# Top-k threshold search of a sparse attention: the count of each search's largest block moved from VectorE to ScalarE

## The chip, the cores and the metric

The kernel runs on one core of a Trainium2 chip. The metric is the device time of one execution in microseconds (us); lower is better. DVE is VectorE, ACT is ScalarE, PE is TensorE, POOL is GpSimd, SP is SyncE with its DMA queue.

## The reference, cut to what matters

Two layers on a sequence of 1024 tokens with 1024 channels in float32. Layer 0 is a sparse attention: an indexer gives each query a score for every key it may see, the 256 best keys are kept, and attention runs over these. Layer 1 is a retention; each layer ends with a gated convolutional FFN. The part that bears on the change:

```python
    topk = min(TOPK_MAX, seq // 4)                                  # 256
    def block(args):
        qb, qib, wb, tb = args
        limit = (tb // CHUNK + 1) * CHUNK
        admissible = key_pos[None, :] < limit[:, None]
        rel = jax.nn.relu(jnp.einsum('bqhd,bsd->bqhs', qib, ki).astype(jnp.float32))
        score = jnp.einsum('bqhs,bqh->bqs', rel, wb.astype(jnp.float32))
        score = jnp.where(admissible[None], score, -jnp.inf)
        _, idx = lax.top_k(score, topk)
        ...
        logits = jnp.where(valid[:, :, None, :], logits, -jnp.inf)
        p = jax.nn.softmax(logits, axis=-1).astype(v_sel.dtype)
        return jnp.einsum('bqhk,bqkd->bqhd', p, v_sel)
```

Equal scores are taken in the order of their index, as `top_k` does.

## The kernel before, in words

Queries lie in 8 blocks of 128 (one per partition); block b sees the first 128 (b + 1) keys. Blocks 0 and 1 see at most 256 keys and need no search. The tokens are worked on in two halves of 512: `in_proj` projects half 0, then half 1, and `indexer` (L369) makes the scores of blocks 2 and 3 beside the first and of blocks 4 to 7 beside the second. Per head and segment of keys it issues two matmuls, a Relu on ACT into a temporary (L380), and a DVE operation that weights it into the score tile `sc` (L383 for the first head, L385 for the others).

`topk` (L391) does not gather. It finds for each query the bits of the 256th largest score: in 31 iterations, from bit 30 to bit 0, every block's scores are compared with the threshold and counted (`count`, L404 to L407: one DVE instruction per block that writes the comparison to `junk` and the sum to `cnt`, with a short accumulator read behind it). Then two small DVE steps on one column per block make the bit (L416, tile `tkb`) and the next threshold (L417, tile `tkt`). One more count stands ahead of the loop (against zero, for the sign, L411) and one behind it (strictly above, L418). The rest (L420 to L429) marks ties by a scan and turns the scores into an additive mask, in place.

There are two searches: a for blocks 2 and 3 (384 and 512 keys), b for blocks 4 to 7 (640, 768, 896 and 1024 keys). Both are generators. A function `steps(n)` advances the first of a list of generators by n yields; the code calls it between projections (`steps((3, 10)[half])`, L268; L246, L255, L332 likewise) for search a, and for search b in the output projection of half 0 (`steps(5)`, L1198) and in the first FFN products (`steps(3)`, L1208). Attention on blocks 0 to 3 (L1196) is written between the two. That is the order in which the code asks for the work. The order in which each engine's queue holds it is made by the framework (`schedule_with_timeline_sim=True`, L1325) from that order, the data dependencies and its own estimate of times; then each engine runs its queue in order.

Weights come by DMA as float32 (`wprep`, L80 to L90), ACT makes their upper half (L87), POOL or DVE the lower half (L89). Matmuls run three times per tile, on halves (`mm3`, L121; `product`, L748). Results in PSUM are split in the same way (`split_psum`, L127: ACT L131 or L134, DVE L132 or L135). POOL also makes the lower halves of squares (L233), inverse square roots (L139) and the scaling of the softmax (L503); the attention's maxima are DVE's (L490), its exponentials ACT's (L501). The sum in `square_sum` (L174), the normaliser (L739) and the FFN's input split (L730, L731) follow the output projection (L552).

Of the kernel before, what the change touches and what calls it, by code (L numbers as in the profile page):

```python
# [5 lines left out]
F32 = mybir.dt.float32  # L6
F32R = mybir.dt.float32r
F16 = mybir.dt.float16
I32 = mybir.dt.int32
AF = mybir.ActivationFunctionType  # L10
ALU = mybir.AluOpType
PSUM = bass.MemoryType.PSUM
# [11 lines left out]
TOPK = 256  # L24
INADM = -3.0e38
MASKED = -1.0e30


C_GMIX = 0
# [22 lines left out]
class Prog:  # L52
# [27 lines left out]
    def wprep(self):  # L80
# [5 lines left out]
        nc.sync.dma_start(raw[:, :n], src)  # L86
        nc.scalar.activation(hi[:, :n], raw[:, :n], AF.Copy)  # L87
        eng = nc.gpsimd if on_pool else nc.vector
# [38 lines left out]
    def split_psum(self, hi, lo, ps, scale=None):  # L127

        nc = self.nc
        if scale is None:  # L130
            i = nc.scalar.activation(hi, ps, AF.Copy)  # L131
            j = nc.vector.tensor_tensor(lo, ps, hi.bitcast(F32), ALU.subtract)  # L132
        else:
            i = nc.scalar.activation(hi, ps, AF.Copy, scale=scale)  # L134
            j = nc.vector.scalar_tensor_tensor(lo, ps, scale, hi.bitcast(F32), op0=ALU.mult, op1=ALU.subtract)  # L135
# [29 lines left out]
    def square_sum(self, x, k):  # L165

        nc = self.nc
        if k == 0:
            self.acc = self.tp.tile([128, 512], F32, tag="acc", bufs=1, name="acc")
            nc.scalar.activation(self.acc, x[:, k], AF.Square)  # L170
        else:
            sq = self.tmp()
            nc.scalar.activation(sq, x[:, k], AF.Square)
            nc.vector.tensor_tensor(self.acc, self.acc, sq, ALU.add)  # L174
# [41 lines left out]
    def in_proj(self, half, hh, hl, steps, also=lambda j, q, qs: None):  # L216
# [10 lines left out]
        def squares(ps):  # L227

            n, w = ps.shape
            sq, hi, lo = self.tmp()[:n, :w], self.tmp(F32R)[:n, :w], self.tmp(F32R)[:n, :w]  # L230
            nc.scalar.activation(sq, ps, AF.Square)
            nc.scalar.activation(hi, sq, AF.Copy)
# [136 lines left out]
    def indexer(self, b, qs, t0, masks):  # L369
        nc = self.nc  # L370
        L = 128 * (b + 1)
        o = 128 * ((b * (b + 1) - 6) // 2)
        masks[b] = sc = self.sc[:, o:o + L]
        for h in range(8):
            for (o, n) in self.segs(L):
                ps = self.bank()
                nc.tensor.matmul(ps[:, :n], qs[:, h, t0:t0 + 128], self.KH[:, o:o + n], start=True, stop=False)
                nc.tensor.matmul(ps[:, :n], qs[:, h, t0:t0 + 128], self.KL[:, o:o + n], start=False, stop=True)
                rl = self.tmp()
                nc.scalar.activation(rl[:, :n], ps[:, :n], AF.Relu)  # L380
                w = self.wr[:, b, h:h + 1]
                if h == 0:
                    nc.vector.tensor_scalar(sc[:, o:o + n], rl[:, :n], w, None, op0=ALU.mult)  # L383
                else:
                    nc.vector.scalar_tensor_tensor(sc[:, o:o + n], rl[:, :n], w, sc[:, o:o + n],  # L385
                                                   op0=ALU.mult, op1=ALU.add)
            if h == 7:
                nc.vector.memset(sc[0:64, L - 64:], INADM)
            yield

    def topk(self, tag, scs, junk, eqs):  # L391

        nc = self.nc
        V = nc.vector
        B = len(scs)
        Ls = [sc.shape[1] for sc in scs]
        sml = lambda n, dt=F32: self.stat.tile([128, B], dt, tag=f"k{n}{tag}", name=f"tk{n}")
        cnt, need = sml("c"), sml("n")  # L400
        bit, thr = sml("b", I32), sml("t", I32)
        t = thr.bitcast(F32)

        def count(of, op):  # L404
            for b in range(B):
                V.tensor_scalar(junk[:, :Ls[b]], scs[b], of(b), None, op0=op, op1=ALU.add, accum_out=cnt[:, b:b + 1])  # L406
                yield  # L407

        yield from count(lambda b: 0.0, ALU.is_ge)  # L411
        V.tensor_scalar(bit, cnt, TOPK - 0.5, -1.0, op0=ALU.is_lt, op1=ALU.mult)
        V.tensor_scalar(thr, bit, 1 << 30, None, op0=ALU.bitwise_xor)
        for k in range(30, -1, -1):
            yield from count(lambda b: t[:, b:b + 1], ALU.is_ge)
            V.tensor_scalar(bit, cnt, TOPK - 0.5, float(1 << k), op0=ALU.is_lt, op1=ALU.mult)  # L416
            V.scalar_tensor_tensor(thr, bit, (1 << k) >> 1, thr, op0=ALU.bitwise_xor, op1=ALU.bitwise_xor)  # L417
        yield from count(lambda b: t[:, b:b + 1], ALU.is_gt)  # L418
        V.tensor_scalar(need, cnt, -1.0, float(TOPK), op0=ALU.mult, op1=ALU.add)
        for b in range(B):  # L420
            nth, eq = junk[:, :Ls[b]], eqs[:, :Ls[b]]
            V.tensor_scalar(eq, scs[b], t[:, b:b + 1], None, op0=ALU.is_equal)
            V.tensor_tensor_scan(nth, eq, eq, 0.0, ALU.add, ALU.max)
            yield
            V.scalar_tensor_tensor(eq, nth, need[:, b:b + 1], eq, op0=ALU.is_le, op1=ALU.mult)
            yield
            V.scalar_tensor_tensor(scs[b], scs[b], t[:, b:b + 1], eq, op0=ALU.is_gt, op1=ALU.add)
            nc.scalar.activation(scs[b], scs[b], AF.Copy, bias=MASKED, scale=-MASKED)
            yield  # L429
# [814 lines left out]
def constants():  # L1244
# [23 lines left out]
    m3 = np.zeros((128, 384), f)  # L1268
    m3[:64, 192:256] = MASKED
    m3[:, 256:] = MASKED  # L1270
    inv = f(1.0) / (f(10000.0) ** (np.arange(0, 256, 2, dtype=f) / f(256)))
# [57 lines left out]
```

## Time and profile before

| | |
|---|---|
| median of 3 runs | 2783.84 us (2782.68 to 2783.91) |
| the profiled execution | 2783.58 us |
| its span | 2781.7 us |
| PE busy | 2655.4 us, 95% |
| DVE busy | 1866.9 us, 67% |
| ACT busy | 1096.2 us, 39% |
| POOL busy | 265.2 us, 10% |
| mean granted clock of PE | 0.976 |

The profile is of one execution. The span runs from the first to the last instruction. Busy time counts an engine's instructions; a share over the whole span mixes stages with different limits, so the rows below go by stretches of time, in us from the span's start. A granted clock of 1.00 is 2.4 GHz, 0.50 is 1.2 GHz. An instruction's line is the line of the kernel that issued it, which may be a helper's.

### The profile page before, as it was taken

Reading aid. Unit: us, or ns where it says so; the run is one execution under the profiler, and the core shown is the slowest. Engines: PE = TensorE matmul, PEld = TensorE weight load, DVE = VectorE, ACT = ScalarE, POOL = GpSimd, SP = SyncE. Lnnn points to the kernel's source line nnn. Section 1 sums busy time; section 2 is a strip of 40 time slices with the busy share of each in tenths; the row PEclk is TensorE's granted clock in tenths of the full one; section 3 lists DMA queues with packets and bytes.
Section 4 is the critical chain, followed back from the end, with each engine's and each line's share of the span. In section 5 each row is a group of like instructions: output and inputs, shape, how many; then the busy total and the mean of one; then the engine's idle time right before and its main releaser. Section 6 shows DMA issues by size and latency. Waiting matters only on the chain.

```text
span 2781.7 us, 31410 instructions
## 1 busy us (share of the span) xinstructions
PE 2655.4 (95%) x11888; PEld 2174.3 (78%) x11888; DVE 1866.9 (67%) x2828; ACT 1096.2 (39%) x1552; POOL 265.2 (10%) x193
## 2 busy tenths in 40 slices
PE   8977789998999999999999999999998999999999
PEld 6755567887788877888888888888886888888887
DVE  6889999765988878744544445445447977777632
ACT  6545424663433333323333343323334554454210
POOL 2543234321000000000000000000000000000000
PEclk9988789999999999999999999999999999999999
DMA  5221035204465575422222223223222433337712
GB/s 196 76 73 53 2 98 182 99 20 138 160 212 189 193 261 176 150 63 90 84 84 87 88 83 122 76 84 98 77 76 84 144 107 108 119 106 286 234 59 87
DMA packets 110343, 328.34 MB, mean 118 GB/s; under 512 B 12400, under 2 KB 13808, under 8 KB 110192
## 3 DMA queue, kind: packets, MB, share of 16 engines
q1 hardware_dynamic: 110192, 326.34, 35.6%
q8 instruction: 93, 1.52, 0.2%
q14 instruction: 58, 0.48, 0.1%
HBM read 250.27 MB, written 72.35 MB: 116 GB/s over the span
## 4 chain that ended last, share of the span: by engine, by line
PE 77%; DVE 15%; DMA 4%; issue 2%; ACT 2%; POOL 0%; SPq 0%; DVEq 0%; ACTq 0%; POOLq 0%
PE bank L753 25%; PE bank L123 17%; PE bank L125 17%; PE bank L124 17%; DVE junk L406 5%; DMA gin<-ud 2%; DVE tkb L416 1%; PE bank L534 1%; DVE sc L385 1%; DVE tkt L417 1%; DMA wraw<-in_wf_up 1%; DVE T L731 1%; DVE wlo L731 1%; DVE xo L764 0%; DVE lg L490 0%
## 5 line engine op out<-in xcount | busy, mean ns | idle before, releaser
L87 ACT ACTIVATE whi<-wraw 128x1024 fp32r<-128x1024 f32 (+1 forms) x194 | 205.3, 1058 | 507.7 <-PE bank L124 262.2
L753 PE MATMUL bank<-T,whi 128*128 128x512 f32 x1072 | 337.5, 396 | 21.6 <-ACT T L730 15.0
L753 PE MATMUL bank<-B,whi 128*128 128x512 f32 x1056 | 328.1, 393 | 11.1 <-ACT B L730 4.1
L89 DVE TENSOR_TENSOR wlo<-wraw,whi 128x1024 fp32r<-128x1024 f32 (+1 forms) x151 | 185.8, 1231 | 214.1 <-ACT whi L87 209.0
L124 PE MATMUL bank<-g,whi 128*128 128x512 f32 x704 | 274.1, 390 | 0.0
L123 PE MATMUL bank<-g,whi 128*128 128x512 f32 x704 | 266.5, 392 | 7.5 <-ACT g L730 5.6
L125 PE MATMUL bank<-g,wlo 128*128 128x512 f32 x704 | 272.5, 390 | 0.5 <-DVE wlo L731 0.5
L753 PEld LDWEIGHTS bank<-T,whi 128*128 128x128 f32 x1072 | 203.8, 190 | 71.0 <-ACT T L730 17.1
L730 ACT ACTIVATE whi<-wraw 128x1024 fp32r<-128x1024 f32 (+2 forms) x153 | 145.1, 949 | 267.0 <-PE bank L124 133.1
L753 PEld LDWEIGHTS bank<-B,whi 128*128 128x128 f32 x1056 | 199.9, 190 | 54.8 <-ACT B L730 4.4
L731 DVE TENSOR_TENSOR wlo<-wraw,whi 128x1024 fp32r<-128x1024 f32 (+2 forms) x153 | 165.7, 1083 | 76.5 <-ACT whi L730 76.3
L753 PE MATMUL bank<-T,wlo 128*128 128x512 f32 x536 | 210.3, 394 | 0.0
L753 PE MATMUL bank<-B,wlo 128*128 128x512 f32 x528 | 205.2, 392 | 0.0
L124 PE MATMUL bank<-wlo,hh 128*128 128x512 f32 x512 | 199.3, 389 | 0.0
L125 PE MATMUL bank<-whi,hl 128*128 128x512 f32 x512 | 199.3, 389 | 0.0
L123 PE MATMUL bank<-whi,hh 128*128 128x512 f32 x512 | 198.7, 390 | 0.0
L123 PE MATMUL bank<-hh,whi 128*128 128x512 f32 (+2 forms) x480 | 188.7, 393 | 10.3 <-ACT hh L134 8.3
L124 PE MATMUL bank<-hl,whi 128*128 128x512 f32 (+2 forms) x480 | 186.5, 389 | 0.1
L125 PE MATMUL bank<-hh,wlo 128*128 128x512 f32 (+2 forms) x480 | 186.4, 389 | 0.0
L406 DVE TENSOR_SCALAR_CACHE_REDUCE junk<-sc,tkt 128x640 f16<-128x640 f32 (+1 forms) x192 | 181.3, 944 | 4.4
L764 DVE TENSOR_TENSOR xo<-xo,bank 128x512 f32<-128x512 f32 x128 | 86.7, 685 | 126.8 <-PE bank L125 126.8
L123 PEld LDWEIGHTS bank<-g,whi 128*128 128x128 f32 x704 | 132.2, 188 | 37.6 <-ACT g L730 7.8
(244 smaller groups left out, 5305.6 us busy)
## 6 DMA issues: line engine op xcount, KB each, us to landing
wraw<-in_wf_up SPq DMA_DIRECT2D x113, 512.0 KB, 3.6
ud<-cu SPq DMA_DIRECT2D x88, 512.0 KB, 2.7
gin<-ud SPq DMA_DIRECT2D x88, 512.0 KB, 4.5
wraw<-in_wb_vg SPq DMA_DIRECT2D x64, 512.0 KB, 3.5
wraw<-in_wf_dn SPq DMA_DIRECT2D x48, 384.0 KB, 3.6
wraw<-in_wb_qk SPq DMA_DIRECT2D x32, 512.0 KB, 3.6
wraw<-in_wb_out SPq DMA_DIRECT2D x32, 512.0 KB, 3.5
wraw<-in_wa_in SPq DMA_DIRECT2D x26, 512.0 KB, 4.0
```

The source lines that it names most:

```text
L87: nc.scalar.activation(hi[:, :n], raw[:, :n], AF.Copy)
L89: eng.tensor_tensor(lo[:, :n], raw[:, :n], hi[:, :n].bitcast(F32), ALU.subtract)
L123: mm(ps, ah, bh, start=first, stop=False)
L124: mm(ps, ah, bl, start=False, stop=False)
L125: mm(ps, al, bh, start=False, stop=last)
L385: nc.vector.scalar_tensor_tensor(sc[:, o:o + n], rl[:, :n], w, sc[:, o:o + n], op0=ALU.mult, op1=ALU.add)
L406: V.tensor_scalar(junk[:, :Ls[b]], scs[b], of(b), None, op0=op, op1=ALU.add, accum_out=cnt[:, b:b + 1])
L416: V.tensor_scalar(bit, cnt, TOPK - 0.5, float(1 << k), op0=ALU.is_lt, op1=ALU.mult)
L730: return (self.nc.scalar.activation(hi, raw, AF.Copy), self.nc.vector.tensor_tensor(lo, raw, hi.bitcast(F32), ALU.subtract))
L731: self.nc.vector.tensor_tensor(lo, raw, hi.bitcast(F32), ALU.subtract))
L753: self.nc.tensor.matmul(ps, u, v, start=first and k + i == 0, stop=k == 3 and i == 2, skip_group_check=not (first and last))
L764: self.nc.vector.tensor_tensor(o, a, b, op)
```

## The change

Search and count stay the same in what they find. For the last block of each search (512 keys in a, 1024 in b) the counts of the iterations k = 30 to 1 come from ACT: the sum over the keys of the sign of (score minus threshold) goes to `half`, and a second ACT instruction makes half of it plus half the number of keys, the count, if no score equals the threshold. To make that so, the scores of this block are turned, in place, into a form with an order that floating-point addition keeps and with the lowest bit set, while its lowest byte's own bit is saved in a byte tile; ahead of k = 0 the bit is put back. The threshold's column for the block holds its negative in these iterations (one XOR on the sign bit ahead, one behind). All scores start from -2^-100 and not from 0. DVE counts the other blocks as before, and all of them for k = 0, ahead of the loop and behind it. The yields per iteration fall by one, while the calls of `steps` stay as they are.

```diff
+SHIFT = -2.0 ** -100
...
-                    nc.vector.tensor_scalar(sc[:, o:o + n], rl[:, :n], w, None, op0=ALU.mult)
+                    nc.vector.tensor_scalar(sc[:, o:o + n], rl[:, :n], w, SHIFT, op0=ALU.mult, op1=ALU.add)
...
+        z, L = B - 1, Ls[B - 1]
+        half = self.stat.tile([128, 1], F32, tag=f"kh{tag}", name="tkh")
+        xi = scs[z].bitcast(I32)
+        x0 = scs[z].bitcast(U8)[:, 0::4]
+        low, signs = eqs.bitcast(U8)[:, :L], eqs.bitcast(I8)[:, 1024:1024 + L]
+
+        def count(of, op, to=B):
+            for b in range(to):
                 V.tensor_scalar(junk[:, :Ls[b]], scs[b], of(b), None, op0=op, op1=ALU.add, accum_out=cnt[:, b:b + 1])
                 yield
...
         yield from count(lambda b: 0.0, ALU.is_ge)
         V.tensor_scalar(bit, cnt, TOPK - 0.5, -1.0, op0=ALU.is_lt, op1=ALU.mult)
         V.tensor_scalar(thr, bit, 1 << 30, None, op0=ALU.bitwise_xor)
+        V.tensor_scalar(thr[:, z:], thr[:, z:], -(1 << 31), None, op0=ALU.bitwise_xor)
+        V.tensor_scalar(low, x0, 1, None, op0=ALU.bitwise_and)
+        yield
+        V.tensor_scalar(xi, xi, 1, None, op0=ALU.bitwise_or)
+        V.scalar_tensor_tensor(xi, xi, 31, xi, op0=ALU.logical_shift_right, op1=ALU.bitwise_xor)
+        yield
         for k in range(30, -1, -1):
-            yield from count(lambda b: t[:, b:b + 1], ALU.is_ge)
+            if k:
+                nc.scalar.activation(signs, scs[z], AF.Sign, bias=t[:, z:], accum_out=half)
+                nc.scalar.activation(cnt[:, z:], half, AF.Copy, bias=L / 2, scale=0.5)
+            yield from count(lambda b: t[:, b:b + 1], ALU.is_ge, B - 1 if k else B)
             V.tensor_scalar(bit, cnt, TOPK - 0.5, float(1 << k), op0=ALU.is_lt, op1=ALU.mult)
             V.scalar_tensor_tensor(thr, bit, (1 << k) >> 1, thr, op0=ALU.bitwise_xor, op1=ALU.bitwise_xor)
+            if k == 1:
+                V.tensor_scalar(thr[:, z:], thr[:, z:], -(1 << 31), None, op0=ALU.bitwise_xor)
+                V.scalar_tensor_tensor(x0, x0, 254, low, op0=ALU.bitwise_and, op1=ALU.bitwise_or)
+                yield
         yield from count(lambda b: t[:, b:b + 1], ALU.is_gt)
```

## Rows read from the trace of the kernel before

**Rows 1.** Stages, us: PE, PEld, DVE, ACT, POOL busy (instructions), granted clock, DMA, GB/s.

```profile
97.00:158.00 61.00, 55.69 (x250) 41.26 (x248) 57.91 (x153) 27.66 (x42) 36.75 (x19) 1.00 0.36 104
158.00:190.00 32.00, 18.38 (x65) 13.52 (x66) 30.22 (x72) 7.26 (x14) 15.92 (x7) 0.68 0.19 58
...
248.00:345.00 97.00, 64.98 (x237) 46.39 (x238) 96.24 (x283) 43.01 (x96) 26.31 (x36) 0.73 0.06 22
345.00:404.00 59.00, 45.94 (x201) 36.58 (x199) 56.99 (x111) 18.79 (x22) 25.62 (x10) 0.90 0.34 107
404.00:520.00 116.00, 110.18 (x486) 91.55 (x487) 99.87 (x177) 49.90 (x77) 42.44 (x21) 0.95 0.47 155
520.00:2781.00 2261.00, 2222.13 (x9988) 1834.93 (x9986) 1414.22 (x1877) 845.10 (x1111) 66.25 (x70) 0.99 0.37 122
```

**Rows 2.** The chain that ended last: share of the span by line.

```profile
PE bank L753 25%; PE bank L123 17%; PE bank L125 17%; PE bank L124 17%; DVE junk L406 5%; DMA gin<-ud 2%; DVE tkb L416 1%; PE bank L534 1%; DVE sc L385 1%; DVE tkt L417 1%; DMA wraw<-in_wf_up 1%; DVE T L731 1%; DVE wlo L731 1%; DVE xo L764 0%; DVE lg L490 0%
```

**Rows 3.** DVE's groups, 97 to 185 us: busy us, mean ns | idle before.

```profile
L406 DVE TENSOR_SCALAR_CACHE_REDUCE junk<-sc,tkt 128x512 f16<-128x512 f32 x32 | 23.9, 746 | 1.0
L406 DVE TENSOR_SCALAR_CACHE_REDUCE junk<-sc,tkt 128x384 f16<-128x384 f32 x32 | 19.6, 612 | 1.0
L416 DVE TENSOR_SCALAR tkb<-tkc 128x2 int32<-128x2 f32 x31 | 17.4, 563 | 1.0
L417 DVE SCALAR_TENSOR_TENSOR tkt<-tkb,tkt 128x2 int32<-128x2 int32 x31 | 13.3, 430 | 1.0
```

**Rows 4.** DVE's groups, 75 to 500 us.

```profile
L406 DVE TENSOR_SCALAR_CACHE_REDUCE junk<-sc,tkt 128x1024 f16<-128x1024 f32 x32 | 40.9, 1277 | 0.5
...
L406 DVE DVE_READ_ACCUMULATOR junk<-sc,tkt 128x1 f32 x192 | 16.0, 83 | 0.0
```

**Rows 5.** ACT's groups over the whole span, by shape; its only two table loads among them.

```profile
L501 ACT ACTIVATION_READ_ACCUMULATOR lg<-lg,s,sq 128x1 f32 x64 | 12.0, 188 | 0.0
...
L335 ACT ACTIVATE q<-bank,cols 128x512 f32<-128x512 f32 x16 | 11.3, 705 | 0.0
...
L501 ACT ACTIVATE lg<-lg,s,sq 128x1024 f32<-128x1024 f32 x8 | 9.9, 1239 | 5.9 <-DVE s L499 5.9
...
L87 ACT ACT_TABLE_LOAD x1 | 1.3, 1283 | 0.7 <-PEq L1322 0.7
L880 ACT ACT_TABLE_LOAD x1 | 1.3, 1283 | 3.4 <-DVE cu L859 3.4
...
L428 ACT ACTIVATE sc<-sc 128x1024 f32<-128x1024 f32 x1 | 1.1, 1062 | 3.9 <-DVE sc L427 3.9
```

**Rows 6.** Timeline of DVE, POOL and ACT: start us, duration us, instruction.

```profile
156.28 0.17 DVE L416 TENSOR_SCALAR tkb<-tkc 128x2 int32<-128x2 f32 x1
...
163.85 2.39 POOL L89 TENSOR_TENSOR wlo<-wraw,whi 128x1024 fp32r<-128x1024 f32 x1
164.20 2.07 DVE L416 TENSOR_SCALAR tkb<-tkc 128x2 int32<-128x2 f32 x1
...
172.22 0.47 ACT L380 ACTIVATE t<-bank 128x384 f32<-128x384 f32 x1
...
178.17 0.42 DVE L383 TENSOR_SCALAR sc<-t,wr 128x384 f32<-128x384 f32 x1
...
250.19 0.88 DVE L406 TENSOR_SCALAR_CACHE_REDUCE junk<-sc,tkt 128x640 f16<-128x640 f32 x1
...
256.52 0.87 DVE L406 TENSOR_SCALAR_CACHE_REDUCE junk<-sc,tkt 128x640 f16<-128x640 f32 x1
```

**Rows 7.** PE's waits, 140 to 190 us: us in total, times, longest.

```profile
PE bank L377 <- ACT t L380: 12.1, 7, 5.9
```

**Rows 8.** PE's waits, 248 to 345 us.

```profile
PE bank L534 <- POOL lg L503: 11.2, 5, 3.0
PE bank L123 <- DVE s L490: 6.4, 7, 1.7
```

**Rows 9.** ACT's waits, 97 to 190 us.

```profile
ACT whi L87 <- DMA wraw<-in_wa_in: 21.0, 5, 6.0
```

More of the change, by code (lines that the diff above doesn't have):

```diff
@@ L9 @@
 I32 = mybir.dt.int32
+I8 = mybir.dt.int8
+U8 = mybir.dt.uint8
 AF = mybir.ActivationFunctionType
@@ L402, in topk @@
         t = thr.bitcast(F32)
-        def count(of, op):
-            for b in range(B):
+        z, L = B - 1, Ls[B - 1]
[5 more added lines that the diff above has]
+            for b in range(to):
                 V.tensor_scalar(junk[:, :Ls[b]], scs[b], of(b), None, op0=op, op1=ALU.add, accum_out=cnt[:, b:b + 1])
```

## The prediction, made before the changed kernel was run

> **What bounds the kernel now.** I read the table of stages first. From 520 us to the end TensorE is busy 2222.13 of 2261 us and its granted clock is 0.99, the full level of 2.4 GHz: nothing that this change touches can shorten that part. From 97 to 520 us it idles, and the clock is a mix of full and half level (1.2 GHz) after stalls: 0.68 in 158 to 190 us, 0.73 in 248 to 345 us [rows 1]. Search a runs in the first two stages of the table, b in the last three before 520; between them, 190 to 248 us, none runs, and that stage is left out. PE's idle time in the five is 5.3, 13.6, 32.0, 13.1 and 5.8 us, together 69.8; what the lower clock costs, estimated as busy time times (1 - clock), is 0, 5.9, 17.5, 4.6 and 5.5, together 33.5. So **103 us is the most** that a change to the searches could bring. In the same stages DVE is nearly full: 57.91 of 61, 30.22 of 32, 96.24 of 97 us [rows 1]. The chain that ended last gives DVE 15% of the span, and its largest DVE piece, 5%, is the count of L406 [rows 2]. That reads as "DVE bounds 97 to 490 us, and counts are most of it". It needs one correction, below.
>
> **What is removed.** Search a has 2 blocks (384 and 512 keys), search b 4 (640 to 1024). In each, the largest block's count leaves DVE for the 30 iterations k = 30 to 1; k = 0, the first and the last count stay. In a 30 x (0.746 + 0.083) = 24.9 us [rows 3, 4]; in b 30 x (1.277 + 0.083) = 40.8 us [rows 4]. Together **65.7 us of DVE**.
>
> **What is added on DVE.** Per search: an OR and a shift-XOR over the whole block as integers, the low byte saved and put back (two byte operations with stride 4), two XORs on one column. No row shows bytes with a stride or 32-bit logic. Bounds at 1024 keys: the count of half the width, 0.746 [rows 3], and the count itself, 1.277 us [rows 4]; I take the upper one for all four, since the count too passes over every key of the block once: 4 x 1.28 + 2 x 0.17 = 5.5 us in b, and by the count of 512 4 x 0.75 + 0.3 = 3.3 us in a. Each may also stand behind POOL, as the small steps do, up to 2.4 us. Sum 8.8 us (5 to 20). The second operation in L383 lies in the same pass: nothing; no row shows it, and at half a count of 512 keys more, 0.37 us, its 10 passes would cost 3.7 us. Net **57 us less DVE work**.
>
> **What is added on ACT.** Sign over 1024 with a pointer bias lies between a Copy with none, 1.062, and an Exp with two, 1.239: 1.15 us. For 512 a one-pointer activation is 0.705. Each also reads its accumulator, 0.188, and rescales one column: between that 0.188, also one column, and the 0.705 of 512 columns; I take 0.19, the nearer row [rows 5]. That makes 1.5 us per iteration in b, 1.1 in a, 78 us over both. ACT has room: 27.66 of 61 us in 97 to 158, 43.01 of 97 in 248 to 345 [rows 1].
>
> **The new wait.** The threshold step now waits for ACT. In b three counts, each longer than the 0.746 us of 512 keys, cover the 1.5 us with at least 0.7 to spare. In a one count, 0.612 + 0.083 [rows 3, 4], covers 1.1 us badly: the trip stands out by 0.4 us. So a's saving of 0.83 per iteration is 0.4 in its own chain, 12 us; the rest is DVE idle time that other work may fill. Behind the waiting step on DVE are the score products L383 and L385 and the lower halves L132 and L135, for which PE waits; behind a Sign on ACT are the splits and Relus.
>
> **What becomes of the 57 us, stage by stage.** Two things take most of it.
> First, **POOL paces the small steps of a**. L416 takes 0.563 us on average and L417 0.430, though such a step takes 0.17 when POOL is idle [rows 6]: (0.39 + 0.26) x 31 = 20 us of waiting [rows 3]. One starts at 164.20 and takes 2.07 us while a POOL subtraction runs from 163.85 for 2.39 us [rows 6]. These steps are as many as before; only what runs beside POOL, the count, gets shorter, so waiting grows. The page "SBUF — State Buffer" of the Trainium skill (SBUF: two separate sides) says that DVE's two-port and two-input operations and GpSimd hold a shared port pair exclusively, for a whole instruction; the trace agrees as to the waiting, and if the port set all of a's pace, a would gain nothing.
> Second, **the queues are filled by the framework, not by program order**: the code asks for search b only from the output projection on, yet its counts run from 250 us, between the attention's operations: the first counts of two iterations follow each other by 6.3 us there, 250.19 and 256.52 [rows 6]. Freed DVE time there is taken by the next iteration's counts.
> - 97 to 158: PE is nearly full, 0.
> - 158 to 190: PE waits 12.1 us for ACT's L380 [rows 7], whose buffers DVE frees late: a Relu starts at 172.22, its product L383 only at 178.17, behind search a, which always has a step ready [rows 6]. With a waiting for ACT, such operations get in. Of 13.6 + 5.9 us I take 8 back (0 to 18).
> - 248 to 345: DVE stays full. An attention operation there waits for half a count, as before; an ACT operation meets a Sign group (1.5 of 6.3 - 1.36 = 4.9 us) 3 times in 10, for half of it, +0.23 us. PE's two largest kinds of wait there are 12 waits, for POOL's share of the softmax and for DVE's maxima [rows 8]: +2.8 us if all grow so. I take +2 (-5 to +12).
> - 345 to 404: projection and normalisation follow each other in series, and the search is not over yet: 0 (-3 to +3).
> - 404 to 520: the search ends some 35 us earlier (40.8 - 5.5), but PE is busy 110.18 of 116 us [rows 1]; of 5.8 + 5.5 us I take 4 back (0 to 8).
> Sum -8 + 2 - 4 = **-10 us**. The profiled execution took 2783.58 us, 1.88 outside its span and 0.26 under the median of 2783.84, so about **2774 us**.
>
> The generators also yield less (72 to 45 in a, 144 to 117 in b), so the calls that step them use them up sooner and put their work further forward; that is in the ranges above.
>
> **Rivals.**
> - *DVE bounds it throughout.* All 57 us, less some for the waits, come off: -45, about 2739. For it: the chain. Against: PE is busy 91 and 95% in the first and the last stage, and fillers refill. 0.10.
> - *Nothing.* Port waits eat a's gain, the fillers b's: 0, 2784 within 5. For it: everything said under "two things". 0.25.
> - *ACT's queue holds the search.* ACT is in order; a Sign behind a weight split waits for what that waits for: 21.0 us in 5 waits for weight DMAs in 97 to 190 us, the longest 6.0 [rows 9]. The threshold step then holds all of DVE. With 60 trips it decides from 57 / 60 = 0.95 us of such wait per trip; at 1.15 us it is +12, about 2796. Against: b's trip has 0.7 us or more in hand. 0.18.
> - *Sign brings table loads.* The kernel has two table loads of 1.283 us, one ahead of the first weight split and one ahead of Silu [rows 5], so one set serves Exp, Square, Relu and Copy. If Sign lay outside it, each change between Sign and Exp in 248 to 345 us, two in each of 97 / 4.9 = 20 iterations, would put 1.283 us on ACT: 51 us, half of it on the path, +25, 2809. The page "ScalarE: Activation LUTs" of the Trainium skill (Table sets: the hidden batching unit) says that functions load in named sets and names the cheap ones that every set has; Sign is not among those it names; no run here shows it yet. 0.05.
> - *The change doesn't do what it says:* both engines write columns of one count tile, and if the framework put them in series, each iteration of b would gain 1.36 and lose 1.5 us, +5 or more in all. 0.02.
>
> **How the numbers follow.** My forecast has 0.40. About 0.2%, 5.6 us, is what a measurement of this kernel tells from no change. Faster: 0.37 of the forecast, 0.10, and 0.04 of "nothing": 0.51. Same: 0.03, 0.21 and 0.02 of the ACT queue: 0.26. Slower: 0.16 + 0.05 + 0.02 = 0.23. The range 2746 to 2800 leaves out the far part of the first rival (0.07), the table loads (0.05) and the far part of the ACT queue (0.05). Within the faster cases alone 2746 to 2778.
>
> **What would show it.** Counts of 512 and 1024 keys down from 32 to 2 each (besides the first, against zero) in DVE's rows, some 60 Signs near 0.7 and 1.15 us on ACT, no further table load; DVE idle before L416 with ACT as its releaser, about 0.4 us each in a, near none in b; PE's wait for L380 well under 12.1 us; the small steps in a no shorter on average; in 248 to 345 us DVE still full and PE's idle time near 32 us; search b some 35 us shorter, with PE no busier after it. I am wrong if PE's idle time in the attention falls by over 10 us, or if DVE stands for ACT by over 1 us per trip.

## The result, and the profile after

The changed kernel takes **2807.55 us** (median of 4 runs), the kernel before 2783.88 beside it: ratio 1.0086, 95% interval 1.0068 to 1.0103. It is 24 us slower; the forecast was 10 us faster. The profiled execution has a span of 2806.2 us against 2781.7, +24.5. Lines of the new kernel stand 4 higher ahead of the search (L174 is L178), 11 to 20 higher inside it (L406 is L417, L416 is L436, L417 is L437) and 24 higher behind it (L552 is L576, L753 is L777). The Sign is L433, the rescale L434.

Part 1 of the page of the changed kernel:

```profile
PE 2660.0 (95%) x11888; PEld 2176.3 (78%) x11888; DVE 1813.9 (65%) x2720; ACT 1159.8 (41%) x1732; POOL 265.7 (9%) x193
```

DVE lost 53.0 us of work, as forecast (57). PE is busy 4.6 us longer (its mean granted clock is 0.974, 0.976 before) and idle 19.9 us longer. The stages of [rows 1], now, and the stretch behind them (start:end, its length, then busy us and instructions of PE, PEld, DVE, ACT, POOL, then clock, DMA share, GB/s):

```profile
97.00:158.00 61.00, 50.05 (x226) 37.23 (x224) 38.55 (x97) 40.24 (x96) 34.54 (x17) 0.98 0.36 104
158.00:190.00 32.00, 22.55 (x88) 17.04 (x86) 23.38 (x65) 19.48 (x47) 18.31 (x8) 0.77 0.20 58
248.00:345.00 97.00, 65.04 (x252) 46.23 (x253) 95.78 (x296) 62.95 (x146) 28.01 (x37) 0.79 0.06 22
345.00:404.00 59.00, 42.02 (x183) 34.53 (x182) 56.48 (x106) 29.46 (x51) 25.57 (x10) 0.86 0.32 107
404.00:520.00 116.00, 103.61 (x438) 83.99 (x438) 66.97 (x97) 48.74 (x73) 35.12 (x15) 0.94 0.44 150
700.00:1200.00 500.00, 478.65 (x2052) 388.89 (x2053) 402.95 (x478) 183.14 (x186) 0.00 (x0) 0.98 0.55 185
```

DVE is still full from 248 to 404 us, so the freed time was filled; DVE's load falls in 97 to 190 us, where it waits, and behind 404 us. The last row is of the FFN, in which no line changed; before it read:

```profile
700.00:1200.00 500.00, 490.66 (x2141) 403.71 (x2142) 402.66 (x476) 180.62 (x185) 0.00 (x0) 0.99 0.57 187
```

PE lost 12 us of busy time there. Stretches at fixed times mix different work once a kernel is late, so I read the starts of the same instructions in both timelines:

| start of | before | after | difference |
|---|---|---|---|
| first product of output projection 0 | 337.65 | 335.67 | -2.0 |
| its last product | 385.90 | 382.48 | -3.4 |
| product of the sum of squares (L180, L184) | 390.24 | 395.16 | +4.9 |
| normaliser's first operation on x | 397.39 | 401.93 | +4.5 |
| first output of the FFN's first products | 411.74 | 417.95 | +6.2 |
| first maximum of the second half's attention | 499.24 | 510.02 | +10.8 |
| last sum of output projection 1 | 650.86 | 663.26 | +12.4 |
| span | 2781.7 | 2806.2 | +24.5 |

The loss has two halves: 12.4 us up to 663 us and 12.1 us behind it. The groups of the search, 75 to 500 us (line, engine, operation, shapes, count, busy us, mean ns of one, idle time before them by releaser):

```profile
L433 ACT ACTIVATE eqs<-sc,tkt 128x1024 int8<-128x1024 f32 x30 | 34.3, 1144 | 28.9 <-DVE tkt L437 27.6 <-DVE s L523 0.9 <-DVE s L527 0.4
L433 ACT ACTIVATE eqs<-sc,tkt 128x512 int8<-128x512 f32 x30 | 21.6, 721 | 24.8 <-DVE tkt L437 21.3 <-DVE tkt L425 3.4
L434 ACT ACTIVATE tkc<-tkh 128x1 f32<-128x1 f32 x60 | 11.7, 196 | 0.9
L433 ACT ACTIVATION_READ_ACCUMULATOR eqs<-sc,tkt 128x1 f32 x60 | 11.2, 186 | 0.0
L436 DVE TENSOR_SCALAR tkb<-tkc 128x2 int32<-128x2 f32 x31 | 15.9, 511 | 24.3 <-ACT tkc L434 24.3
L436 DVE TENSOR_SCALAR tkb<-tkc 128x4 int32<-128x4 f32 x31 | 15.3, 495 | 1.1
```

The counts of 512 and 1024 keys went from 32 to 2 each, the 60 Signs take what was forecast, and DVE waits for ACT in search a only, 24.3 us in 24 waits. Over the whole span the table loads are still two [rows 5]:

```profile
L91 ACT ACT_TABLE_LOAD x1 | 1.3, 1283 | 0.7 <-PEq L1346 0.7
L904 ACT ACT_TABLE_LOAD x1 | 1.3, 1283 | 3.1 <-DVE cu L883 3.1
```

Where PE stood in 345 to 410 us (waits: us in total, times, the longest):

```profile
PE bank L184 <- DVE acc L178: 12.3, 1, 12.3
PE bank L777 <- ACT B L754: 3.8, 1, 3.8
PE bank L777 <- DVE B L755: 3.4, 1, 3.4
PE bank L149 <- POOL rms L143: 1.3, 1, 1.3
```

The first one read, in the kernel before:

```profile
PE bank L180 <- DVE acc L174: 4.0, 1, 4.0
```

PE ends the output projection earlier than before, then waits for a sum of squares that DVE makes late. DVE's timeline there, changed kernel (start, duration):

```profile
383.43 1.22 DVE L436 TENSOR_SCALAR tkb<-tkc 128x4 int32<-128x4 f32 x1
384.57 0.68 DVE L576 TENSOR_TENSOR x<-x,bank 128x512 f32<-128x512 f32 x1
...
389.07 1.59 DVE L436 TENSOR_SCALAR tkb<-tkc 128x4 int32<-128x4 f32 x1
390.70 0.16 DVE L437 SCALAR_TENSOR_TENSOR tkt<-tkb,tkt 128x4 int32<-128x4 int32 x1
390.90 0.88 DVE L417 TENSOR_SCALAR_CACHE_REDUCE junk<-sc,tkt 128x640 f16<-128x640 f32 x1
...
391.70 0.68 DVE L576 TENSOR_TENSOR x<-x,bank 128x512 f32<-128x512 f32 x1
392.30 1.01 DVE L417 TENSOR_SCALAR_CACHE_REDUCE junk<-sc,tkt 128x768 f16<-128x768 f32 x1
...
393.35 1.15 DVE L417 TENSOR_SCALAR_CACHE_REDUCE junk<-sc,tkt 128x896 f16<-128x896 f32 x1
394.42 0.08 DVE L417 DVE_READ_ACCUMULATOR junk<-sc,tkt 128x1 f32 x1
394.42 0.69 DVE L178 TENSOR_TENSOR acc<-acc,t 128x512 f32<-128x512 f32 x1
```

The last two sums L576 stand a whole trip of search b apart, at 384.57 and 391.70, though PE had started its last product at 382.48; two more counts stand between the last one and its square's sum L178.

In 663 to 1212 us PE's waits for operands that ACT splits are longer, and new ones for DVE and ACT have come (changed kernel, then before):

```profile
PE bank L127 <- ACT g L754: 10.1, 3, 5.9
PE bank L777 <- DVE wb L755: 2.7, 3, 1.6
PE bank L777 <- ACT wb L754: 1.8, 1, 1.8
PE bank L777 <- DVE cu L788: 1.7, 2, 0.8
```

```profile
PE bank L123 <- ACT g L730: 5.1, 3, 2.6
```

The reason is in the compiled queues. Compared instruction by instruction, DVE, ACT and PE hold this FFN's work in another order than before. The framework orders each queue by its estimate of the whole program, and a change in the search moves that estimate.

### The profile page after: what moved, and what is told of

The parts are those of the page before. It is cut to its first block, busy times and chain, and to the rows that moved or that the text cites. A ratio compares the mean times of both kernels' runs of the same rounds, so it can differ in the third digit from the quotient of the medians.

```text
span 2806.2 us, 31557 instructions
## 1 busy us (share of the span) xinstructions
PE 2660.0 (95%) x11888; PEld 2176.3 (78%) x11888; DVE 1813.9 (65%) x2720; ACT 1159.8 (41%) x1732; POOL 265.7 (9%) x193
## 4 chain that ended last, share of the span: by engine, by line
PE 75%; DVE 15%; DMA 4%; ACT 3%; issue 3%; POOL 0%; SPq 0%; DVEq 0%; ACTq 0%
PE bank L777 23%; PE bank L127 17%; PE bank L129 16%; PE bank L128 16%; DVE junk L417 3%; DMA gin<-ud 2%; DMA wraw<-in_wf_up 1%; DVE tkb L436 1%; DVE wlo L755 1%; PE bank L558 1%; DVE sc L389 1%; ACT eqs L433 1%; DVE T L755 1%; DVE tkt L437 1%; DVE t L788 1%
## 5 line engine op out<-in xcount | busy, mean ns | idle before, releaser
L91 ACT ACTIVATE whi<-wraw 128x1024 fp32r<-128x1024 f32 (+1 forms) x194 | 204.5, 1054 | 460.9 <-PE bank L128 236.4
L777 PE MATMUL bank<-T,whi 128*128 128x512 f32 x1072 | 337.5, 396 | 20.2 <-ACT T L754 14.2
L777 PE MATMUL bank<-B,whi 128*128 128x512 f32 x1056 | 329.0, 394 | 15.3 <-ACT t L833 5.3
L777 PEld LDWEIGHTS bank<-T,whi 128*128 128x128 f32 x1072 | 203.7, 190 | 69.1 <-ACT T L754 16.4
L777 PEld LDWEIGHTS bank<-B,whi 128*128 128x128 f32 x1056 | 199.9, 190 | 59.6 <-ACT t L833 6.4
L777 PE MATMUL bank<-T,wlo 128*128 128x512 f32 x536 | 210.4, 393 | 0.3 <-DVE wlo L755 0.3
L777 PE MATMUL bank<-B,wlo 128*128 128x512 f32 x528 | 205.2, 392 | 0.4 <-POOL wlo L93 0.4
L129 PEld LDWEIGHTS bank<-g,wlo 128*128 128x128 f32 x704 | 132.3, 188 | 28.5 <-DVE wlo L755 0.8
```

The source lines that it names most:

```text
L129: mm(ps, al, bh, start=False, stop=last)
L777: self.nc.tensor.matmul(ps, u, v, start=first and k + i == 0, stop=k == 3 and i == 2, skip_group_check=not (first and last))
```

## The experiments

All times are medians; ratios are against the kernel before, run beside them on the same chip.

### One search alone; the FFN's order alone

Runs e1 and e2, `on = tag == 'a'` or `'b'`:

```diff
-            if k:
+            if k and on:
                 nc.scalar.activation(signs, scs[z], AF.Sign, bias=t[:, z:], accum_out=half)
...
-            yield from count(lambda b: t[:, b:b + 1], ALU.is_ge, B - 1 if k else B)
+            yield from count(lambda b: t[:, b:b + 1], ALU.is_ge, B - 1 if k and on else B)
```

Runs e3 (on the changed kernel) and e4 (on the kernel before):

```diff
+                nc.vector.tensor_copy(self.kon[:, K_CAUS:K_END], self.kon[:, K_CAUS:K_END])
+                nc.vector.tensor_copy(self.kon[:, K_CAUS:K_END], self.kon[:, K_CAUS:K_END])
                 x, h = self.ffn_first(x, tt, s3)
```

> Signs on ScalarE in search a alone; search b counts all its blocks on DVE as before the change. Theory order (the loss comes from the small operations of the normalisation and the output projection that stand in DVE's and ScalarE's queues behind b's new trips, and as much again from another order of the queues in the stage after 700 us, which is not touched): 2784 to 2789 us, 0 to +5. Rival wait (DVE standing for ScalarE in a's trips, 24.3 us of it in the changed kernel, delays what is behind it and causes most of the loss): +10 us or more, 2794 to 2800.

> Signs on ScalarE in search b alone. Theory order: nearly all of the loss is here, 2803 to 2807 us (+19 to +24), with PE's wait for DVE's sum of squares near 12 us and the stage from 700 to 1200 us some 12 us longer than before. Rival wait: the smaller part, +5 to +14 us, 2789 to 2798.

> The changed kernel with two copies of a small constant onto itself on DVE ahead of the first feed-forward stage; with them its queues in that stage stand in the order that the kernel before has. Theory order: the part of the loss that arises after 700 us goes, 2795 us (2793 to 2798), with the milestones up to 663 us (end of the second output projection) as in the changed kernel. Rival wait: what is lost after 700 us only follows from what was lost before, so 2806 to 2809 us.

> The kernel before with the same two copies, which leave its queues in their order. Both theories: the time of the kernel before, 2783 to 2786 us; if the copies themselves moved the time, the run before this one could not be read.

Measured: e1 2786.87 us (1.001, 1.0001 to 1.002), e2 2806.85 (1.0084, 1.0069 to 1.0099), e3 2792.72 (1.0034, 1.002 to 1.0048), e4 2782.74 (0.9994, 0.9985 to 1.0003). All four come out by theory order (e3 and e4 lie 0.3 us below their ranges): search b holds nearly all of the loss, and two copies that compute nothing bring 14.8 us back from the changed kernel while they cost the kernel before nothing. In e3 the FFN's waits are again those of before:

```profile
PE bank L127 <- ACT g L754: 4.2, 2, 2.7
```

What stays in e3 is 8.3 to 9 us, with the wait for the sum of squares still at 12.3 us.

### What the first half's loss is made of

e5 (on e3) and e6 (on the kernel before) do not form the low half of the weights for the output projection of half 0 and use the high half twice. That leaves out a part of the computation, keeps PE's work, and takes away GpSimd's eight subtractions for this projection:

```diff
-                seq += [(i["wa_out"][m], 1024, a == 0) for m in range(8)]
+                seq += [(i["wa_out"][m], 1024, None if a == 0 else False) for m in range(8)]
...
-        eng.tensor_tensor(lo[:, :n], raw[:, :n], hi[:, :n].bitcast(F32), ALU.subtract)
+        if on_pool is None: lo = hi
+        else: eng.tensor_tensor(lo[:, :n], raw[:, :n], hi[:, :n].bitcast(F32), ALU.subtract)
```

On the kernel before, e7 has the relief without its price (the largest block's threshold is not searched for), e8 the price without the relief (the Signs' result is read by nobody), e9 both without a wait between them. The diff is e9's; e7 leaves the three lines at `if k` out, e8 has these alone:

```diff
+        V.memset(thr[:, z:], 1 << 30); V.memset(cnt[:, z:], 0.0)
         for k in range(30, -1, -1):
+            if k:
+                nc.scalar.activation(signs, scs[z], AF.Sign, bias=t[:, z:], accum_out=half)
+                nc.scalar.activation(spare, half, AF.Copy, bias=L / 2, scale=0.5)
-            yield from count(lambda b: t[:, b:b + 1], ALU.is_ge)
+            yield from count(lambda b: t[:, b:b + 1], ALU.is_ge, B - 1 if k else B)
```

> The kernel of the run with the two copies, and in the first output projection the low part of each weight is not formed (its high part is used twice, so that part of the computation is left out; TensorE's work stays). GpSimd then subtracts nothing while the sums and squares of that projection are made. Theory port (search b's small steps stand behind GpSimd's subtractions there, 0.9 to 1.6 us each, and stretch each trip, and with it every sum that stands between two trips): small steps of 0.17 us, TensorE's wait for the sum of squares down from 12.3 to 5 to 7 us, 2785 to 2788 us, 5 to 8 under that run. Rival ScalarE (squares come late behind Signs): wait still 11 to 12 us, 2791 to 2794 us.

> The kernel before with the same low parts not formed (the same part of the computation left out). Both theories: 2781 to 2784 us, 0 to -3: its wait for the sum of squares was 4.0 us and only one small step in that projection stood long (2.14 us).

> The kernel before with the counts of the largest block left out of the 30 iterations in both searches (its threshold is then not searched for; that part of the computation is left out), nothing added on ScalarE or DVE: the relief of DVE alone, 65.7 us. Theory port: little of it reaches TensorE, 2772 to 2784 us (-12 to 0), since small steps and sums stand as before and what is behind the search is bound by TensorE. Rival DVE bounds: about 2739 us (-45).

> The kernel before, DVE counting all blocks, with the Signs and the rescale on ScalarE as well, into a column that nobody reads: ScalarE's load alone, and no wait for it. Theory port: 2784 to 2789 us (0 to +5), the small steps being no later than before. Rival ScalarE (squares, splits and Relus stand behind Signs, which is most of what search b loses up to 520 us): +6 to +12, 2790 to 2796 us.

> The relief of DVE and the load of ScalarE together, and no wait between them: the counts of the largest block are left out of the 30 iterations (its threshold is not searched for), the Signs and the rescale run on ScalarE, into a column that nobody reads. Its queues after 700 us stand as in the kernel before. Theory coupling (neither part costs anything, the loss up to 520 us is DVE's threshold step waiting for ScalarE's in-order queue and ScalarE's squares and splits for DVE's): 2780 to 2786 us. Rival (both loads together are too much for the two queues, wait or no wait): 2790 to 2794 us, as in the run with the two copies.

Measured: e5 2789.48 us (1.0022, 1.0013 to 1.0032), e6 2779.82 (0.9986, 0.9977 to 0.9996), e7 2781.79 (1.0003, 0.9992 to 1.0014), e8 2784.65 (1.0006, 0.9996 to 1.0015), e9 2788.89 (1.0019, 1.001 to 1.0028).

**e7 is the main answer to the forecast**: 65.7 us of counts taken from DVE, at no price anywhere, move the time by nothing that can be told. Its stages 248 to 345 and 345 to 404 us show where those of search b went:

```profile
248.00:345.00 97.00, 69.51 (x255) 49.16 (x256) 94.19 (x293) 42.51 (x96) 27.76 (x37) 0.74 0.07 22
345.00:404.00 59.00, 46.16 (x190) 37.02 (x189) 56.78 (x115) 18.75 (x22) 24.25 (x10) 0.86 0.32 107
```

DVE is as full as before. By 389 us search b had done 25 threshold steps in e7, 23 in the changed kernel, 19 before: the time became further trips. Search a's relief is worth nothing either, though no filler took it: a's last threshold step starts at 151.11 us, not 178.50, and DVE is then busy for only 13.76 of 32 us in 158 to 190. But PE waits 8.1 us for the ACT operation L277, which stands in ACT's queue behind a's first mask step, and that waits for DVE:

```profile
158.36 0.53 ACT L453 ACTIVATE sc<-sc 128x384 f32<-128x384 f32 x1 [6.36 <-DVE sc L452]
158.79 0.57 ACT L277 ACTIVATE t<-bank 10x512 f32<-10x512 f32 x1
```

e8 shows that 78 us more on ACT cost nothing that can be told either. Both together without a wait, e9, cost 4.7 us, between what the theory and its rival said: some half of e3's 8 to 9 us needs no wait at all. The attention of the first half gains in all three: the first product of the output projection starts at 334.40, 334.95 and 330.26 us, against 337.65. Only e7 keeps some of that, 2.0 us: the product of the sum of squares starts at 388.19, 391.08 and 390.14, against 390.24.

e5 shows the port theory half right. Its text says that GpSimd subtracts nothing there; in the trace three subtractions for the next stage's weights remain, at 373.57, 379.01 and 387.91 us. None of the six steps L436 (L437 here) between 360 and 392 us falls beside one of them, and a step takes 165 ns and not 1056 as in e3. What falls beside one instead is stretched in its turn, the last square's sum from 0.69 to 1.70 us:

```profile
387.91 2.35 POOL L94 TENSOR_TENSOR wlo<-wraw,whi 128x1024 fp32r<-128x1024 f32 x1 [6.50 <-ACT whi L91]
389.11 1.70 DVE L179 TENSOR_TENSOR acc<-acc,t 128x512 f32<-128x512 f32 x1
```

PE's wait falls all the same:

```profile
PE bank L185 <- DVE acc L179: 7.6, 1, 7.6
```

That is 4.7 us less (a wait of 5 to 7 us was expected), and the normaliser starts 5.1 us earlier than in e3. But the end moved by 3.2 us only, and the control e6 by 3.7: of the time at the end nothing can be credited to it.

### Signs in a part of search b

e10 and e11 are e2 with Signs for k = 30 to 10 and 30 to 12, e14 for k = 30 to 14:

```diff
-            if k and on:
+            if k >= 10 and on:
...
-            if k == 1 and on:
+            if k == 10 and on:
```

> Search b alone, and Signs only for k = 30 to 10, 21 of its trips, most of which run inside the attention of the first half; DVE counts all blocks from k = 9. Its queues after 700 us stand as in the kernel before. Theory coupling: the attention's gain (its first sum of the output projection 7 us earlier in the run with Signs in search b alone) stays and the loss in the output projection and after it goes, 2776 to 2782 us (-8 to -2). Rival (the gain of the attention is given back at the next series step whatever is done): 2783 to 2787 us.

> As the run before, two trips less on ScalarE (k = 30 to 12), but with this one number the queues after 700 us stand in the order of the changed kernel. Theory order: 11 to 15 us over the run before, 2788 to 2796 us, with TensorE's wait for ScalarE's g near 10 us in that stage. Rival (the order of the queues there costs nothing by itself): within 3 us of the run before.

> Signs in search b for k = 30 to 14, DVE counts all blocks from k = 13, nothing held. Its queues after 700 us stand in a third order, the one of the run before. If that order costs nothing, the time of the run with k = 30 to 10, 2783 to 2787 us; if it costs what the changed kernel's order costs, 2795 us or more.

Measured: e10 2785.53 us (1.0006, 0.9997 to 1.0015), e11 2792.72 (1.0032, 1.0019 to 1.0044), e14 2797.23 (1.0046, 1.0031 to 1.0061). e10 is the rival's result: the attention's gain is given back. Two of these texts name the orders wrongly: in the compiled queues e11 has a third order after 700 us (its wait for g is 5.4 us, not near 10), and e14, e13 and e2 have the changed kernel's there (e12 and e15 nearly so). By that, e14 is the cleanest proof of the order's price. It is level with the kernel before at the last sum of output projection 1 (650.86 before):

```profile
650.11 0.69 DVE L577 TENSOR_TENSOR x<-x,bank 128x512 f32<-128x512 f32 x1 [1.53 <-PE bank L129]
```

Its span is 2795.0, so 14.0 us are lost behind that point, and in 663 to 1212 us it has the changed kernel's waits, first of all:

```profile
PE bank L127 <- ACT g L755: 10.2, 3, 5.5
```

How late each kernel is against the kernel before, at that sum and at the end of the span:

| order after 700 us | kernels: late there, late at the end (us) |
|---|---|
| as before | e1 5.1, 4.5; e3 10.5, 8.3; e4 1.0, -0.3; e5 7.0, 6.6; e6 -1.3, 0.5; e7 -1.3, -1.5; e8 -0.8, -1.8; e9 2.5, 3.1; e10 3.6, 2.1 |
| as in the changed kernel, or nearly | changed 12.4, 24.5; e2 8.2, 21.8; e12 4.8, 15.6; e13 12.3, 26.2; e14 -0.8, 13.3; e15 1.7, 14.9 |
| a third | e11 5.2, 9.1 |

With the order of before the lateness moves by -2.2 to +1.8 us on the way to the end; with the changed kernel's it grows by 10.8 to 14.1, whatever the search does. That is the second half of the loss. e4, the kernel before with two idle copies, shows how much of a figure in this table is chance: some 1 us.

### The search held back

To see what keeps the sums late, search b waits by a true dependence. On e2 (e12), on the changed kernel (e13) and on the kernel before (e15):

```diff
         for k in range(30, -1, -1):
...
+            if tag == 'b' and k == 14:
+                yield 'hold'
+                V.scalar_tensor_tensor(cnt, self.acc[:, :B], 0.0, cnt, op0=ALU.mult, op1=ALU.add)
...
+                next(v for v in gb if v == 'hold')
-                x[0] = self.out_proj(0, *ot, lambda m: steps(5))
+                x[0] = self.out_proj(0, *ot)
+                gens.append(gb)
```

> Signs in search b alone, and search b held after 17 trips until the last sum of squares of the output projection is made: its 17th threshold step takes in that sum times zero, and the projection no longer steps the search. Theory filling: the product of the sum of squares starts 3 to 5.5 us after the projection's last product (12.7 us in the run with Signs in b alone), so near 384 us instead of 392, DVE no longer full in 345 to 404 us; the search ends near 490 us; 2776 to 2782 us. Rival (the sums are late for another reason): 8 us or more after the last product, 2784 us or more.

> The changed kernel (Signs in both searches) with search b held in the same way. Theory filling: the product of the sum of squares near 388 us instead of 396, first attention operation of the second half near 502 us instead of 510, and 2782 to 2788 us, 20 under the changed kernel, some 13 of it by the order of the queues after 700 us if that order costs nothing. Rival: product near 396 us, 2790 us or more.

> The kernel before, DVE counting all blocks, with search b held in the same way. Theory filling: the product of the sum of squares 0 to 2 us earlier than at 390.2 us (its sums were late by 4.3 us only), but the search ends later, at 505 to 520 us instead of 490, and the second half's attention waits for it: 2786 to 2800 us. Rival (holding the search costs nothing even so): 2781 to 2784 us.

Measured: e12 2800.63 us (1.0064, 1.0047 to 1.0081), e13 2809.29 (1.0088, 1.0073 to 1.0103), e15 2800.45 (1.006, 1.0045 to 1.0075). The wait for the sum of squares is as theory filling had it, the times are not: all three lie above their ranges. In e12, and with the same 3.9 us in e13, the wait for the sum of squares is down to before's size, with DVE busy only 39.89 of 59 us in 345 to 404:

```profile
PE bank L184 <- DVE acc L178: 3.9, 1, 3.9
```

| start of | before | changed | e2 | e5 | e9 | e12 | e13 |
|---|---|---|---|---|---|---|---|
| last product of output projection 0 | 385.90 | 382.48 | 379.74 | 382.89 | 377.46 | 379.99 | 382.84 |
| product of the sum of squares | 390.24 | 395.16 | 392.42 | 390.86 | 390.14 | 384.31 | 387.17 |
| between them | 4.3 | 12.7 | 12.7 | 8.0 | 12.7 | 4.3 | 4.3 |

So trips of search b ahead of the sums make them late, shown by taking the trips away; of 8.4 us too much, e5 puts 4.7 or more on steps that stand behind GpSimd's subtractions. But e12 gives it back in the next stage: 6.3 us ahead of the kernel before at the normaliser (391.08), it is 4.6 us behind at the first maximum of the second half (503.88). The trips that were held run there, and in 404 to 520 us PE's outputs stand behind the search on ACT, 6.9 of these 7.5 us behind mask steps:

```profile
PE bank L781 <- ACT t L837: 7.5, 4, 3.8
```

The whole kernels lose besides by the order after 700 us, e15 nearly all of its loss: it is 1.7 us late at the last sum of output projection 1 and 14.9 at the end. And e13, 8.0 us ahead of the changed kernel at the product of the sum of squares, is level with it at the last sum of output projection 1 (663.14 against 663.26) and has its time. The wait for the sum of squares is thus explained, but what it alone costs in the end is not shown: holding the search moves the price into the next stage.

## Why the prediction was wrong

**What held.** The counts removed, net DVE work (57 forecast, 53.0 measured), the Signs (1.15 and 0.705 forecast, 1.144 and 0.721 measured), with their reads and rescales 78.8 us by the groups (78 forecast), nothing for the second operation in L383 (476 ns for 512 keys, 467 before), no wait of DVE for ACT in b, no table load. Two rivals fall by that: the table loads, and the ACT queue that holds the search, which needed 57 us of DVE's waiting and got 24.3. That the change does not do what it says falls too. Sign is not among the functions that the page "ScalarE: Activation LUTs" of the Trainium skill (Table sets: the hidden batching unit) names as in every set; these runs show it in the set of Exp. In a the wait was mis-sized: 24.3 us over 30 trips is 0.8 us each, not 0.4.

**The relief.** "DVE bounds it throughout" is refuted by e7. The second of the "two things", that freed DVE time there is taken by the next iteration's counts, is right for b, and e7 shows that the whole relief was worth nothing: the price of the change should have been weighed against a gain of 0, not of 10.

**97 to 158 us: 0, and 158 to 190 us: -8.** The step that failed is "With a waiting for ACT, such operations get in". The product L383 does get in sooner, 1.1 us after its Relu and not 6 [rows 6], but that Relu now starts at 180.80 us and not at 172.22. PE's wait for the Relu fell from 12.1 [rows 7] to 9.1 us, and two others grew in its place:

```profile
PE bank L381 <- ACT t L384: 9.1, 4, 7.0
PE bank L282 <- ACT t L277: 6.3, 1, 6.3
PE bank L229 <- ACT t L236: 4.6, 2, 3.2
```

PE's waits for ACT in 97 to 190 us come to 20.0 us, against 14.2 before (12.1, 1.7 and 0.4); by 158 us, where the text had put 0, it is 10.9 against 1.7, and PE is busy for 5.6 us less. The working priced the splits and Relus behind a Sign in b alone (+0.23 us each), and put nothing for them in a, where a Sign also waits for DVE. L277 started at 147.27 us before (L273 there) and now stands behind two such Signs:

```profile
154.64 0.72 ACT L433 ACTIVATE eqs<-sc,tkt 128x512 int8<-128x512 f32 x1 [2.64 <-DVE tkt L437]
...
156.18 0.72 ACT L433 ACTIVATE eqs<-sc,tkt 128x512 int8<-128x512 f32 x1 [0.49 <-DVE tkt L437]
...
156.90 0.57 ACT L277 ACTIVATE t<-bank 10x512 f32<-10x512 f32 x1
```

Nor did a's own chain get 12 us shorter. It got 7 us longer: its first and last threshold steps start at 97.46 and 185.57 us, before at 97.19 and 178.50. e1 prices the whole of search a: 2.5 us slower.

**248 to 345 us: +2.** Better than forecast, at the lower end of its range (-5) or just past it: in e2, with search a as before, the first product of the output projection starts 6.0 us earlier. The clock rose from 0.73 to 0.79.

**345 to 404 us: 0 (-3 to +3).** This failed by about 8 us (from 3.4 early at the projection's last product to 4.5 late at the normaliser). "Projection and normalisation follow each other in series" was read as cover; it is the place where an operation that stands behind a search trip goes straight onto the path. Nothing in the working asked how many trips stand between two sums, and where the small steps fall against GpSimd's subtractions: ACT's split L91 follows the rescale in its queue, GpSimd's subtraction follows that, and the next threshold step then stands behind it, 1.06 us on average. The exclusive port pair of the page "SBUF — State Buffer" of the Trainium skill (SBUF: two separate sides), which the forecast weighed for search a alone, agrees with e5: the steps that fall beside no subtraction take 165 ns, the sum that falls beside one 1.70 us and not 0.69.

**404 to 520 us: -4 (0 to 8 back).** The search did end 27 us earlier (its last mask step starts at 463.37, was 490.17), and it was worth less than nothing: +6.3 us from normaliser to the second half's attention. From the one to the other PE runs the same 395 matmuls in each kernel (before, changed, e12):

```profile
397.39:499.24 101.85, 93.83 (x395) 76.74 (x396) 93.30 (x143) 39.80 (x54) 35.46 (x14) 0.93 0.45 147
401.93:510.02 108.09, 95.17 (x395) 76.75 (x396) 62.40 (x81) 43.60 (x64) 35.07 (x14) 0.92 0.43 148
391.08:503.88 112.80, 98.32 (x395) 77.25 (x396) 95.45 (x144) 53.11 (x88) 34.85 (x14) 0.91 0.43 142
```

In the changed kernel it idles there for 12.9 us, not 8.0, and is busy 1.3 us longer. It waits 5.3 us for outputs (3.0 before) behind mask steps on ACT, and its clock is 0.65 in 404 to 420 us (0.85 before).

**Behind 520 us.** This is the largest failure. "Nothing that this change touches can shorten that part" is true and was used as if it also meant "or lengthen". The text knew that the framework fills the queues from its own estimate, and drew that consequence for the search's neighbourhood alone. e3 gives the term that was missing 14.8 us, e14 14.0.

**The yields.** "Put their work further forward" is refuted without a run: with one yield more per trip, and with `steps(5)` set to 0, 2, 3 or 8 in e3, DVE's queue is the same, instruction for instruction.

**The signs to look for.** Neither of the two that were to show the forecast wrong came up (PE's idle time in the attention fell by 0.1 us, DVE stood 0.8 us per trip): both looked at the search, and the loss lay in what stands behind it. Of the signs for it one failed: the small steps of a were to be no shorter, and they are (511 and 295 ns on average, 563 and 430 before [rows 3]), so the text's growing wait for POOL did not come.

**Open.** Why the framework's order after 700 us turns on so little (two copies, or k = 14 instead of 10) was not found, nor a version that keeps e14's search with the order of before; by the table, an estimate, such a version would be level with the kernel before, not ahead of it. In e9 the 4.7 us are not split further. No kernel here beats the one before by more than the measurement can tell, but for e6, which leaves work out.

## What to carry to other kernels

Before moving work off a full engine, ask what fills the time it frees: where a search, a prefetch or any other filler stands ready, it takes the relief (b), and where none does, another engine's wait may (a). Dropping the work outright (e7) prices that in one run. Look at the short serial steps between two stages first, and count what stands in the queue ahead of each, on the engine that takes the work over too. Where a framework orders the queues, compare the queues of the whole program, also where no line changed: here the order of an untouched stage cost 14 us, more than all else.

## What the runs showed of the hardware

A small DVE step can take six to ten times its usual time without any wait in the profile: 128x4 in 165 ns with no GpSimd subtraction beside it (e5), 1057 ns on average in the same stretch with them, 1.59 us at 389.07 in the changed kernel (above) beside this subtraction on GpSimd's timeline:

```profile
388.30 2.34 POOL L93 TENSOR_TENSOR wlo<-wraw,whi 128x1024 fp32r<-128x1024 f32 x1 [3.67 <-ACT whi L91]
```

A DVE operation on every fourth byte of 1024 keys took 1.367 us, 32-bit logic over 1024 keys 1.212 us, both about a count's 1.28. Here PE's waits are paid a second time in the clock (the figure ahead of the DMA share). Behind 12.3 us in 383 to 395 us, and the three shorter waits up to 410, it is 0.65 in 404 to 420 us, a mix of half and full level. In the kernel before it falls too, behind a first wait of 4.0 us, but is back sooner, 0.85 in the same 16 us (changed kernel, then before):

```profile
404.00:420.00 16.00, 12.07 (x38) 9.20 (x39) 15.54 (x29) 7.46 (x12) 0.00 (x0) 0.65 0.04 15
404.00:420.00 16.00, 15.97 (x61) 13.04 (x62) 15.51 (x29) 3.97 (x6) 2.31 (x1) 0.85 0.16 59
```
